# Forget sums and the causal mask of branch B move from TensorE to VectorE; the shift's weights and the key stacks are spread

## The chip, the cores and the metric

One core of one Trainium2 chip runs the whole kernel. The metric is the device time of the execution in microseconds (us); lower is better. The time before is 2265.0 us, the median of three runs.

## The reference

A pool-mixer block is followed by a hybrid layer of three attention branches: A (sliding window, 12 heads), B (forgetting attention, 12 heads) and C (attention over 256 memory tokens, 4 heads). There are 512 tokens, the width is 2048, and everything is fp32. Cut to what matters:

```python
def first_block(x, c, w_mod, b_mod, pool_w_in, pool_w_grp, pool_scale, pool_w_out, ...):
    shift, scale, gate = ada_modulation(c, w_mod[i], b_mod[i])   # silu(c) @ w_mod + b_mod, in three parts
    h = rms_norm(x) * (1.0 + scale) + shift
    y = pool_mixer(h, pool_w_in[j], pool_w_grp[j], pool_scale[j], pool_w_out[j])
    x = x + gate * y
    return rms_norm(x) * final_norm_g
...
def forgetting_attention(q, k, v, f_logit, q_gain, k_gain):       # branch B, 12 heads of 64
    log_f = jax.nn.log_sigmoid(f_logit.astype(jnp.float32))
    c = jnp.cumsum(log_f, axis=1).transpose(0, 2, 1)
...
    def block_fn(args):
        sc = jnp.einsum('bqhd,bshd->bhqs', qb, k) * scale + cqb[..., None] - c[:, :, None, :]
        mask = key_pos[None, :] <= qpos[:, None]
        sc = jnp.where(mask[None, None], sc, NEG)
        p = jax.nn.softmax(sc, axis=-1)
        return jnp.einsum('bhqs,bshd->bqhd', p, v)
...
def hybrid_layer(x, mem, ...):
    proj = rms_norm_2(x, norm_gain) @ w_in
    ua = (sliding_window_attention(...) * silu(za)) @ w_branch_a
    ub = (forgetting_attention(...) * silu(zb)) @ w_branch_b
    uc = (memory_attention(...) * silu(zc)) @ w_branch_c
    g = sigmoid(gate_logits)
    return x + (g0 * ua + g1 * ub + g2 * uc) @ w_out
```

For B the score of a query and a key is their product, plus the query's running sum of log forget values, minus the key's, with all later keys masked out. The query's sum is the same for all keys of one softmax row.

## The kernel before

Every fp32 product is made of three matmuls on split numbers: a weight piece of 128 x 512 comes from memory as `raw`, ScalarE casts it to `whi` (line 91), VectorE subtracts to get `wlo` (line 92), and TensorE multiplies high by high, high by low and low by high (`mm3`, all through line 257). All weights go through one stream (`Stream`): a list of entries (`plan`), loaded in order by SyncE into 3 `raw` buffers of 512 KB. Half an entry is one piece. Four `whi`/`wlo` pairs exist, two more are lent in the first third of the program, and `take` keeps two pieces ready ahead of the one being used (four while the pairs are lent). Entries with a key are not split: VectorE multiplies them by `csil` and adds them up (`gemv`, `shift_part`, `gate_part`).

The order of all engines is the program order, written out by hand. The main loop (`tile_steps`) calls `step()` after every three matmuls of a piece (about 0.7 us); a projection of 8 tiles has 64 such steps. `step` adds a rate to a credit, and each whole credit runs a side generator on to its next `yield` (an advance). `drain()` runs what is left of it at once. So attention is a generator beside the projections of the next heads: `attend` for C, for A (two units of 6 heads) and for B (three units of 4 heads), each beside two projections (for the last B unit beside the first two gate tiles) at a rate of 0.4 (0.34 for C).

A B unit runs in this order. `silu_z`; `head_norm` (9 advances, with a Sqrt on ScalarE); four stacks (`transp_stack`, lines 879 to 894), two of queries and two of keys, each an advance: four transposes into a PSUM bank, then ScalarE and VectorE write high and low halves from the same bank. The bank alternates (`S4[2 + nside % 2]`); before the first B unit 18 stacks and splits have gone by, so a B unit's four stacks take banks s2, s3, s2, s3. Then come 12 items, three to a head, with 128 + 256, 384 and 512 key columns. Item `e` has `s0(e)` in one advance (scores in bank s0 or s1: two matmuls for the products, one with `cs` and `mov` for both forget sums, one with `idr` and `dmr` for the mask; VectorE takes the row maximum, line 1078; ScalarE does the Exp straight from PSUM, line 1083) and `s2(e)` three advances later (transposes of `pt` into bank s2; ScalarE writes `pth`, VectorE `ptl`, lines 1130 and 1132). After a head's last item `s4` multiplies by the values into bank s3, `release` (lines 1023, 1024) reads that bank one advance later at the start of the next loop pass, ahead of `s0`, `finish` scales, and `flush` transposes the finished pair of heads into the score bank that the next item uses.

Ahead of attention: the modulation. `mod` loads the scale part of `w_mod`, VectorE adds it up (line 441), and the first `w_pin` tiles wait for it. The 32 entries of the shift part (`plan_shift`, 512 KB each, line 653) stand in the plan behind those tiles: 2, and then 2 behind every `w_pin` tile of groups 2 and 3. `begin_shift` needs the last of them in the last tile of group 3. At lines 812 to 828 the pool `a3` opens, and its small constants are loaded and copied.

## Time and profile before

| | us |
|---|---|
| three runs | 2263.77, 2265.0, 2267.54 |
| median | 2265.0 |
| profiled execution, its time | 2263.53 |
| its span in the trace | 2261.7 |
| TensorE busy | 2211.3 |
| VectorE busy | 1146.0 |
| ScalarE busy | 873.4 |
| mean granted TensorE clock | 0.993 |

The span is the time from the first to the last instruction of the profiled execution; 1.8 us of its time lie outside of it. Matmuls overlap in the records, so a busy TensorE may still run late: the start of one matmul to the start of the next is the better measure, and 178 or 179 matmuls of 512 columns in 40 us is what it does undisturbed.

### The profile page before, as it was taken

To read this page: it belongs to the slowest core of one execution; us is meant where nothing else is said; L and a number is where in the kernel's file an instruction comes from. 1 tells how busy PE (TensorE), PEld (TensorE's weight loads), DVE (VectorE), ACT (ScalarE), POOL (GpSimd) and SP (SyncE) were. 2 spreads that over 40 slices of the span, in tenths; PEclk is the share of its full clock that TensorE was granted. 3 is DMA by queue.
4 is the path that set the end of the run, shared out by engine and by line. 5 is a ranking of instruction groups with operands and counts; after the bars stand their busy time and mean duration, and the time that the engine had idled before them with its cause. 6 is when DMAs were issued, how large, how long until landed. Compare 5 with 4: busy or idle time off the path is not lost.

```text
span 2261.7 us, 26823 instructions
## 1 busy us (share of the span) xinstructions
PE 2211.3 (98%) x10199; PEld 1820.7 (80%) x10199; DVE 1146.0 (51%) x1996; ACT 873.4 (39%) x1707; POOL 0.2 (0%) x4
## 2 busy tenths in 40 slices
PE   7999999999999999999999999999999999999999
PEld 4678788888888988888878787788888888888887
DVE  3655675436665354657564645554334235326332
ACT  4432263333334353545454546442232222224221
POOL 0000000000000000000000000000000000000000
PEclk9999999999999999999999999999999999999999
DMA  9836743336764332222222222233333333333443
GB/s 328 279 102 199 239 122 111 94 121 225 226 220 126 101 91 75 75 75 75 75 75 75 75 75 75 66 96 100 93 93 102 96 101 93 102 95 98 154 131 112
DMA packets 164665, 275.12 MB, mean 122 GB/s; under 512 B 11074, under 2 KB 62776, under 8 KB 164280
## 3 DMA queue, kind: packets, MB, share of 16 engines
q1 hardware_dynamic: 164536, 273.41, 39.6%
q8 instruction: 80, 1.31, 0.2%
q14 instruction: 49, 0.40, 0.1%
HBM read 264.98 MB, written 8.39 MB: 121 GB/s over the span
## 4 chain that ended last, share of the span: by engine, by line
PE 82%; DVE 7%; DMA 6%; ACT 4%; issue 2%; SPq 0%; ACTq 0%; DVEq 0%
PE m L257 54%; PE s L257 25%; DMA raw<-w_pin 2%; DVE wlo L92 1%; DVE qk L893 1%; DMA raw<-w_kv 1%; ACT whi L91 1%; PE s L1105 1%; DMA raw<-w_pout 1%; ACT pt L1083 1%; ACT qk L889 1%; DMA raw<-w_mod 1%; DVE acc L441 1%; DVE nm L1076 1%; DVE pt L1074 0%
## 5 line engine op out<-in xcount | busy, mean ns | idle before, releaser
L92 DVE TENSOR_TENSOR wlo<-raw,whi 128x512 fp32r<-128x512 f32 (+2 forms) x740 | 493.2, 675 | 770.9 <-ACT whi L91 761.2
L91 ACT CAST whi<-raw 128x512 fp32r<-128x512 f32 (+2 forms) x740 | 441.0, 608 | 878.5 <-PE m L257 385.4
L257 PE MATMUL m<-whi,h_h 128*128 128x512 f32 (+2 forms) x960 | 372.8, 388 | 4.4 <-ACT whi L91 2.9
L257 PE MATMUL m<-wlo,h_h 128*128 128x512 f32 (+2 forms) x960 | 362.2, 377 | 2.1 <-DVE wlo L92 2.0
L257 PE MATMUL m<-whi,h_l 128*128 128x512 f32 (+2 forms) x960 | 362.6, 378 | 0.0
L257 PE MATMUL m<-h_h,whi 128*128 128x512 f32 x768 | 305.8, 398 | 4.9 <-ACT up L549 3.4
L257 PE MATMUL m<-h_h,wlo 128*128 128x512 f32 x768 | 302.6, 394 | 2.2 <-DVE wlo L92 2.2
L257 PE MATMUL m<-h_l,whi 128*128 128x512 f32 x768 | 302.2, 393 | 0.0
L257 PEld LDWEIGHTS m<-whi,h_h 128*128 128x128 f32 x960 | 180.9, 188 | 31.9 <-ACT whi L91 3.4
L257 PEld LDWEIGHTS m<-whi,h_l 128*128 128x128 f32 x960 | 180.6, 188 | 31.6
L257 PEld LDWEIGHTS m<-wlo,h_h 128*128 128x128 f32 x960 | 181.1, 189 | 28.6 <-DVE wlo L92 2.9
L257 PE MATMUL s<-h_h,wlo 128*128 128x512 f32 x512 | 200.1, 391 | 0.0
L257 PE MATMUL s<-h_h,whi 128*128 128x512 f32 x512 | 200.0, 391 | 0.0
L257 PE MATMUL s<-h_l,whi 128*128 128x512 f32 x512 | 200.0, 391 | 0.0
L257 PEld LDWEIGHTS m<-h_h,whi 128*128 128x128 f32 x768 | 146.2, 190 | 35.5 <-ACT up L549 3.8
L257 PEld LDWEIGHTS m<-h_h,wlo 128*128 128x128 f32 x768 | 146.1, 190 | 34.4 <-DVE wlo L92 3.0
L257 PEld LDWEIGHTS m<-h_l,whi 128*128 128x128 f32 x768 | 146.4, 191 | 29.8
L257 PEld LDWEIGHTS s<-h_h,whi 128*128 128x128 f32 x512 | 96.7, 189 | 20.1
L257 PEld LDWEIGHTS s<-h_l,whi 128*128 128x128 f32 x512 | 96.5, 189 | 20.1
L257 PEld LDWEIGHTS s<-h_h,wlo 128*128 128x128 f32 x512 | 96.5, 189 | 20.1
L257 PE MATMUL m<-whi,y_h 128*128 128x512 f32 x256 | 102.6, 401 | 1.7 <-DVE t L777 1.7
L257 PE MATMUL m<-whi,y_l 128*128 128x512 f32 x256 | 99.9, 390 | 0.0
(237 smaller groups left out, 2731.2 us busy)
## 6 DMA issues: line engine op xcount, KB each, us to landing
raw<-w_mod SPq DMA_DIRECT2D x96, 512.0 KB, 4.6
raw<-w_in SPq DMA_DIRECT2D x96, 512.0 KB, 3.8
raw<-w_pin SPq DMA_DIRECT2D x58, 512.0 KB, 3.7
raw<-w_in SPq DMA_DIRECT2D x96, 256.0 KB, 3.1
raw<-w_pout SPq DMA_DIRECT2D x32, 512.0 KB, 4.4
raw<-w_out SPq DMA_DIRECT2D x32, 512.0 KB, 3.7
raw<-w_in SPq DMA_DIRECT2D x32, 384.0 KB, 3.4
raw<-w_kv SPq DMA_DIRECT2D x16, 512.0 KB, 6.9
```

Of the source, the lines that this page charges most:

```text
L91: self.nc.scalar.copy(h3, v)
L92: self.nc.vector.tensor_tensor(out=l3, in0=v, in1=h3.bitcast(F32), op=ALU.subtract)
L257: PE.matmul(ps, lhsT=lhsT, rhs=rhs, start=start, stop=stop)
L441: V.scalar_tensor_tensor(out=acc, in0=v[:, e, :], scalar=w, in1=acc, op0=mult, op1=add)
L889: S.activation(hi[r, :], b[r, :], AF.Copy, scale=gain[r, :])
L893: V.scalar_tensor_tensor(out=outs[e][1][w, :], in0=b[r, :], scalar=gain[r, :], in1=r32(hi[r, :]), op0=mult, op1=sub)
L1076: V.tensor_reduce(out=s["nm"][:, qt : qt + m], in_=w, axis=AX.X, op=vmax)
L1083: S.activation(pt[:, c0 : c0 + n], (pt if kind == "A" else b)[:, c0 : c0 + n], AF.Exp, bias=s["nm"][:, qt : qt + 1], accum_out=s["den"][:, ...
L1105: PE.transpose(b[:, x * P : (x + 1) * P], pt[:, c : c + P], idf)
```

## The change

- B's two score matmuls for the sums and the mask are gone. VectorE adds the key's sums (`sums`) to the scores as it takes them out of PSUM, and the mask (`dmf`) to the last 128 columns; maximum and Exp then read `pt` in SBUF. The query's sum is left out, since it cancels in the softmax.
- The key's sums come once per head from one 128 x 512 matmul (`key_sums`, bank s3) with a column selector (`pick`), copied to SBUF by ScalarE. `key_sums(0)` has an advance of its own behind the stacks; `key_sums(h + 1)` is issued in `s0` of a head's last item. The copies to `idr`, `dmr` and the scaled `cs` (line 967) are gone, and `ct2` with them.
- A key stack takes two advances in place of one. `flush` moves from the second to the first advance of a loop pass, ahead of `finish`, and one advance earlier. The rate is 0.41 in place of 0.4 for A and B.
- `silu_z` ends with an Exp on one column.
- The shift's 32 entries are spread: 10 behind the first `w_pin` tiles, 2 behind the strided entries, 10 in group 2, 10 in group 3. The accumulators move to a pool that lives longer, and `xr` takes their place later.

```diff
@@ -145,9 +145,6 @@
     for kp in range(8):
         for c in range(2):
             ent(w_kv, kp, [(512 * c, 512, 0)])
-    for kp in range(8):
-        ent(w_pin, kp, [(0, 512, 0)])
-        ent(w_pin, kp, [(512, 384, 0)], n=384)
 
     shifts = [(k, c) for k in range(NK) for c in range(2)]
 
@@ -156,24 +153,28 @@
             ent(w_mod, 0, [(1024 * c, 1024, 0)], n=1024, kc=1, row0=k * P, key=("s", c, k))
         del shifts[:n]
 
+    for kp in range(8):
+        ent(w_pin, kp, [(0, 512, 0)])
+        ent(w_pin, kp, [(512, 384, 0)], n=384)
+        plan_shift((0, 0, 1, 1, 2, 2, 2, 2)[kp])
     for r in range(2):
         ent(w_pin, 0, [(896, 128, 0)], n=128, kc=8, row0=1024 * r)
-    plan_shift(2)
+        plan_shift(1)
 
 
     GRP = {2: {2: (0, 0), 5: (0, 1)}, 3: {2: (1, 0), 5: (1, 1)}, 4: {3: (2, 0), 6: (2, 1)}, 5: {3: (3, 0), 6: (3, 1)}}
 
-    def plan_group(w, segs, n=512, grp={}, gate=None, shift=0):
+    def plan_group(w, segs, n=512, grp={}, gate=None, shift=None):
         for kp in range(8):
             if gate is not None:
                 ent(w_mod, kp, [(4096 + 512 * gate, 512, 0)], key=("g", gate, kp))
             ent(w, kp, segs, n=n)
-            plan_shift(shift)
+            plan_shift(shift[kp] if shift else 0)
             if kp in grp:
                 ent(w_grp, 0, [(0, 512, 0)], row0=512 * grp[kp][0] + 256 * grp[kp][1])
 
     for g in range(2, 8):
-        plan_group(w_pin, [(512 * g, 512, 0)], grp=GRP.get(g, {}), shift=2)
+        plan_group(w_pin, [(512 * g, 512, 0)], grp=GRP.get(g, {}), shift={2: (2, 1, 1, 1, 2, 1, 1, 1), 3: (2, 1, 2, 1, 2, 1, 1, 0)}.get(g))
     for cg in range(4):
         plan_group(w_pout, [(512 * cg, 512, 0)], gate=cg)
     CG = [(5120, 346), (5466, 346), (5812, 344)]
@@ -329,6 +330,16 @@
     xnT = [xq[k // 4][:, k % 4, :] for k in range(NK)]
     st.lend(yhs.enter_context(tc.tile_pool(name="hlx", bufs=2)))
 
+    sacc = [yhp.tile([P, 1024], F32, tag=f"sacc{c}", name=f"sacc{c}") for c in range(2)]
+
+    def shift_part(c, k, v):
+        w, v = csil[:, k : k + 1], v[:, 0, :]
+        if k == 0:
+            V.tensor_scalar(out=sacc[c], in0=v, scalar1=w, scalar2=None, op0=mult)
+        else:
+            V.scalar_tensor_tensor(out=sacc[c], in0=v, scalar=w, in1=sacc[c], op0=mult, op1=add)
+
+
     p0 = ExitStack()
     a0 = p0.enter_context(tc.tile_pool(name="a0", bufs=1))
     mod = Stream(nc, mod_plan, p0.enter_context(tc.tile_pool(name="gp", bufs=9)), None, 9, 0)
...
@@ -643,16 +654,6 @@
                     pool[0] = new_pool(i + cp, 1 - cp)
 
 
-    sacc = [a1.tile([P, 1024], F32, tag=f"sacc{c}", name=f"sacc{c}") for c in range(2)]
-
-    def shift_part(c, k, v):
-        w, v = csil[:, k : k + 1], v[:, 0, :]
-        if k == 0:
-            V.tensor_scalar(out=sacc[c], in0=v, scalar1=w, scalar2=None, op0=mult)
-        else:
-            V.scalar_tensor_tensor(out=sacc[c], in0=v, scalar=w, in1=sacc[c], op0=mult, op1=add)
-
-    more["s"] = shift_part
     shf = a1.tile([P, NK], F32, name="shf")
 
     shifted = [0]
@@ -785,7 +786,9 @@
             if kp == 6:
                 drain()
                 for tt in range(NT):
-                    xr = a2.tile([P, 512], F32, tag=f"xr{tt}", name="xr")
+                    if tt % 2 == 0:
+                        two = yhp.tile([P, 2, T], F32, tag=f"sacc{tt // 2}", name="xr")
+                    xr = two[:, tt % 2, :]
                     nc.sync.dma_start(xr, x[tt * P : (tt + 1) * P, cg * 512 : (cg + 1) * 512])
                     xrs.append(xr)
             if kp == 7:
@@ -811,16 +814,12 @@
     ur = [uraw_p.tile([P, T], F32, tag=f"ur{k}", name=f"ur{k}") for k in range(NK)]
     p3 = ExitStack()
     a3 = p3.enter_context(tc.tile_pool(name="a3", bufs=1))
-    idr = a3.tile([P, P], F32R, name="idr")
-    S.copy(idr, idf)
     dmf = a3.tile([P, P], F32, name="dmf")
     nc.sync.dma_start(dmf, dmask)
-    dmr = a3.tile([P, P], F32R, name="dmr")
-    S.copy(dmr, dmf)
     rels = a3.tile([P, 256], F32, name="rels")
     nc.sync.dma_start(rels, rel)
-    csl = a3.tile([P, 12], F32, name="csl")
-    nc.sync.dma_start(csl, csel)
+    ckl = a3.tile([P, 12], F32, name="ckl")
+    nc.sync.dma_start(ckl, csel)
     snk = a3.tile([P, 12], F32, name="snk")
     nc.sync.dma_start(snk, sinks.partition_broadcast(P))
     bfg = a3.tile([P, 12], F32, name="bfg")
@@ -891,14 +890,14 @@
                 S.activation(hi[o, :], b[r, :], AF.Copy, scale=gain[r, :])
             for w in ((r, o) if keys else (o,)):
                 V.scalar_tensor_tensor(out=outs[e][1][w, :], in0=b[r, :], scalar=gain[r, :], in1=r32(hi[r, :]), op0=mult, op1=sub)
-        yield
+            if e or keys:
+                yield
 
     qk12 = a3.tile([P, 12, T], F32R, name="qk12")
     qkh, qkl = qk12[:, 0:6, :], qk12[:, 6:12, :]
     vhl = a3.tile([P, 2048], F32R, name="vhl")
 
     mov = a3.tile([P, T], F32R, name="mov")
-    ct2 = a3.tile([P, T], F32R, name="ct2")
 
     def forget(qk):
         lf = a3.tile([P, 512], F32, tag="pt", name="lf", bufs=2).rearrange("p (t h) -> p t h", t=NT)
...
@@ -930,12 +929,9 @@
         for tt in range(NT):
             mm(b[:, tt * P :], lf[:, tt, :], trs[:, : T - tt * P], start=tt == 0, stop=tt == NT - 1)
         yield
-        V.memset(r32(mov), 1.0)
-        V.memset(r32(ct2), 1.0)
+        V.memset(r32(mov), 0.0)
         S.copy(mov[0:64, :], b[0:64, :])
         V.tensor_tensor(out=mov[32:64, :], in0=b[32:64, :], in1=r32(mov[32:64, :]), op=sub)
-        S.copy(ct2[64:128, :], b[64:128, :])
-        V.tensor_tensor(out=ct2[96:128, :], in0=b[96:128, :], in1=r32(ct2[96:128, :]), op=sub)
         yield
 
     def split_v(srcs, dst, d):
@@ -954,6 +950,8 @@
         def silu_z():
             z = vz[:, :, zoff : zoff + nh * d]
             S.activation(z, z, AF.Silu)
+            t = a3.tile([P, 1], F32, tag="tab", name="tab", bufs=2)
+            S.activation(t, ones[:, 0:1], AF.Exp)
 
         hs = {}
 
@@ -962,13 +960,27 @@
                 s = {}
                 s["nm"] = a3.tile([P, NT], F32, tag="nm", name="nm", bufs=3)
                 s["den"] = a3.tile([P, NT], F32, tag="den", name="den", bufs=3)
-                if kind == "B" and "cs" not in s:
-                    s["cs"] = a3.tile([P, T], F32R, tag="cst", name="cst", bufs=2)
-                    S.activation(s["cs"], r32(ct2), AF.Copy, scale=csl[:, h0 + h : h0 + h + 1])
                 hs[h] = s
             return hs[h]
 
+        sel, sums = {}, {}
+
+        def pick(h):
+
+            sel[h] = a3.tile([P, P], F32R, tag="sel", name="sel", bufs=2)
+            S.activation(sel[h], ones, AF.Copy, scale=ckl[:, h0 + h : h0 + h + 1])
+
+        def key_sums(h):
+
+
+            b = bank("s3")
+            mm(b, sel.pop(h), mov, start=True, stop=True)
+            sums[h] = a3.tile([P, T], F32, tag="cst", name="cst", bufs=2)
+            S.copy(sums[h], b)
+
         head_state(0)
+        if kind == "B":
+            pick(0)
 
         if kind == "C":
             vv = vhl.rearrange("p (m h e) -> p m h e", m=2, h=4)
@@ -1056,12 +1068,13 @@
                     mm3(bb, qkh[:, h, qs], qkl[:, h, qs], kch[:, h, ks], kcl[:, h, ks], True, True)
                 else:
                     mm(bb, qk12[:, h, qs], kh[:, ks], start=True)
-                    mm(bb, qk12[:, h, qs], kl[:, ks], stop=kind != "B")
-                if kind == "B":
-                    mm(bb, s["cs"][:, qs], mov[:, :n])
-                    mm(b[:, c0 + n - P : c0 + n], idr, dmr, stop=True)
+                    mm(bb, qk12[:, h, qs], kl[:, ks], stop=True)
             if segs[0][0] == 0 and h + 1 < nh:
                 head_state(h + 1)
+                if kind == "B":
+                    pick(h + 1)
+            if kind == "B" and segs[-1][0] == NT - 1 and h + 1 < nh:
+                key_sums(h + 1)
             pt = a3.tile([P, 512], F32, tag="pt", name="pt", bufs=2)
             its[e] = pt
             q0, nq = segs[0][0], len(segs)
@@ -1074,13 +1087,19 @@
                     V.scalar_tensor_tensor(out=w, in0=rels[:, 256 - n :].unsqueeze(1).to_broadcast([P, m, n]), scalar=SLOPES[h0 + h],
                                            in1=v, op0=mult, op1=add)
                     V.tensor_reduce(out=s["nm"][:, qt : qt + m], in_=w, axis=AX.X, op=vmax)
+                elif kind == "B":
+                    w = pt[:, c0 : c0 + m * n]
+                    V.tensor_tensor(out=w, in0=b[:, c0 : c0 + m * n], in1=sums[h][:, :n], op=add)
+                    dg = pt[:, c0 + n - P : c0 + n]
+                    V.tensor_tensor(out=dg, in0=dg, in1=dmf, op=add)
+                    V.tensor_reduce(out=s["nm"][:, qt : qt + m], in_=w, axis=AX.X, op=vmax, negate=True)
                 else:
                     V.tensor_reduce(out=s["nm"][:, qt : qt + m], in_=v, axis=AX.X, op=vmax, negate=True)
             if kind == "A":
                 nm = s["nm"][:, q0 : q0 + nq]
                 V.tensor_scalar(out=nm, in0=nm, scalar1=snk[:, h0 + h : h0 + h + 1], scalar2=-1.0, op0=vmax, op1=mult)
             for qt, c0, n in segs:
-                S.activation(pt[:, c0 : c0 + n], (pt if kind == "A" else b)[:, c0 : c0 + n], AF.Exp, bias=s["nm"][:, qt : qt + 1],
+                S.activation(pt[:, c0 : c0 + n], (b if kind == "C" else pt)[:, c0 : c0 + n], AF.Exp, bias=s["nm"][:, qt : qt + 1],
                              accum_out=s["den"][:, qt : qt + 1])
 
 
@@ -1159,25 +1178,28 @@
 
             for q in pend:
                 q[2] += 1
-            if pend and (force or pend[0][2] > 1):
+            if pend and (force or pend[0][2] > 0):
                 un, chunk, _, os = pend.pop(0)
                 b = bank(S4[(e + 1) % 2])
                 for tt in range(NT):
                     PE.transpose(b[:, tt * P : (tt + 1) * P], un[:, tt, :], idf)
                 V.tensor_tensor(out=ur[chunk], in0=b, in1=os, op=mult)
 
+        if kind == "B":
+            key_sums(0)
+            yield
         ne = len(items)
         for e in range(ne + 2):
             for h in later:
                 release(h)
             if e < ne:
                 s0(e)
+            flush(e)
             while later:
                 finish(later.pop(0))
             yield
             if e >= 2:
                 s4(e - 2)
-            flush(e)
             if 1 <= e <= ne:
                 s2(e - 1)
             yield
@@ -1254,7 +1276,7 @@
         proj(qk2, False)
         vz2 = new_vz()
         proj(vz2, True)
-        aside(attend(kind, unit, qk2, vz2), 0.4)
+        aside(attend(kind, unit, qk2, vz2), 0.41)
 
 
     p4 = ExitStack()
...
```

## Rows read from the trace of the kernel before

**Rows 1.** The page's list of engines: busy us (share of the span) x instructions.
```profile
PE 2211.3 (98%) x10199; PEld 1820.7 (80%) x10199; DVE 1146.0 (51%) x1996; ACT 873.4 (39%) x1707; POOL 0.2 (0%) x4
```

**Rows 2.** The view by windows, three stretches of 40 us: group 2 to group 3 of the pool block, the start of the last B unit, and the gate tiles. Columns: stretch, length, busy us (x instructions) of each engine, granted clock, DMA share, GB/s.
```profile
240.00:280.00 40.00, 36.59 (x154) 29.72 (x153) 26.51 (x29) 12.06 (x21) 0.00 (x0) 0.96 0.72 232
...
1360.00:1400.00 40.00, 36.77 (x164) 29.29 (x163) 26.13 (x49) 23.69 (x46) 0.00 (x0) 0.91 0.28 78
1520.00:1560.00 40.00, 40.00 (x179) 33.10 (x178) 21.13 (x32) 9.12 (x15) 0.00 (x0) 1.00 0.36 104
```

**Rows 3.** The view of waits, TensorE, whole span: who waited for whom, us in total, times, longest.
```profile
PE colb L257 <- DVE acc L441: 7.3, 6, 2.7
...
PE s L257 <- DVE ur L1167: 3.3, 2, 1.6
```

**Rows 4.** The timeline of TensorE in the second B unit: start us, us, instruction, count. Scores of a head's first item (128 and 256 columns), of its last item (512 columns), and of the next head's last item.
```profile
1265.80 0.28 PE L257 MATMUL s<-mov,cst 128*128 128x128 f32 x1
...
1266.02 0.46 PE L257 MATMUL s<-qk 128*128 128x256 f32 x2
1266.31 0.28 PE L257 MATMUL s<-mov,cst 128*128 128x256 f32 x1
...
1266.49 0.45 PE L257 MATMUL m<-whi,h_h 128*128 128x512 f32 x1
...
1280.35 0.39 PE L257 MATMUL s<-mov,cst 128*128 128x512 f32 x1
...
1280.64 0.45 PE L257 MATMUL m<-whi,h_h 128*128 128x512 f32 x1
...
1295.39 0.39 PE L257 MATMUL s<-mov,cst 128*128 128x512 f32 x1
```

**Rows 5.** The timeline around the end of group 2, TensorE and ScalarE, and the group of the shift's sums on VectorE in the view by lines from 178 to 306 us (busy us, mean ns, idle before).
```profile
247.87 0.39 PE L257 MATMUL m<-h_h,wlo 128*128 128x512 f32 x1
251.67 0.50 PE L257 MATMUL m<-h_h,whi 128*128 128x512 f32 x1 [3.41 <-ACT up L549]
...
249.99 1.14 ACT L91 CAST whi<-raw 128x512 fp32r<-128x512 f32 x2 [3.53 <-DMA raw<-w_pin]
...
L653 DVE SCALAR_TENSOR_TENSOR sacc<-raw,csil,sacc 128x1024 f32<-128x1024 f32 x30 | 37.8, 1281 | 8.4 <-DMA raw<-w_mod 8.4
```

**Rows 6.** The timeline where the pool `a3` opens: ScalarE's copy of the mask, and TensorE's next matmul behind it.
```profile
726.18 0.30 ACT L819 CAST dmr<-dmf 128x128 fp32r<-128x128 f32 x1 [2.57 <-DMA dmf<-dmask]
...
726.91 0.43 PE L257 MATMUL m<-whi,h_h 128*128 128x346 f32 x1 [1.41 <-ACT whi L91]
```

**Rows 7.** The view by lines, ScalarE's table loads ahead of a Sqrt (L310) and of the first Exp of an attention unit (L1083): count, busy us, mean ns, idle before.
```profile
L310 ACT ACT_TABLE_LOAD x8 | 10.3, 1283 | 0.1
L1083 ACT ACT_TABLE_LOAD x8 | 10.3, 1283 | 5.8 <-DVE nm L1078 5.8
```

**Rows 8.** The view of waits, TensorE, 1127 to 1470 us (the three B units).
```profile
PE s L1105 <- ACT pt L1083: 5.4, 3, 3.5
PE m L257 <- ACT whi L91: 2.9, 2, 1.5
PE m L257 <- DVE wlo L92: 2.1, 2, 1.2
```

**Rows 9.** The timeline at the start of the second B unit: transposes of its last key stack, the first scores, the last piece of that stack on ScalarE and VectorE, and TensorE's transposes of the first `pt`.
```profile
1263.53 0.60 PE L885 MATMUL s<-idf,qk 128*128 128x128 f32 x4
...
1265.36 0.60 PE L257 MATMUL s<-qk 128*128 128x128 f32 x2
...
1270.85 0.68 ACT L889 ACTIVATE qk<-s,cols 64x512 fp32r<-64x512 f32 x1 [1.81 <-DVE qk L893]
...
1272.26 1.53 DVE L893 SCALAR_TENSOR_TENSOR qk<-s,cols,qk 64x512 fp32r<-64x512 f32 x2 [1.45 <-ACT qk L891]
...
1276.31 1.15 PE L1105 MATMUL s<-idf,pt 128*128 128x128 f32 x3 [3.49 <-ACT pt L1083]
```

**Rows 10.** The items of the second B unit, 1280 to 1340 us (four heads): the stretch in the view by windows (columns as in group 2), then groups of the view by lines for VectorE and ScalarE; the last two groups are branch A's scores plus bias, taken from PSUM, in 1015 to 1127 us.
```profile
1280.00:1340.00 60.00, 60.00 (x313) 50.97 (x312) 34.00 (x78) 29.96 (x82) 0.00 (x0) 1.00 0.26 76
...
L92 DVE TENSOR_TENSOR wlo<-raw,whi 128x512 fp32r<-128x512 f32 x18 | 12.3, 691 | 10.5 <-ACT whi L91 10.2
L1132 DVE TENSOR_TENSOR ptl<-s,pth 128x128 fp32r<-128x128 f32 x24 | 7.0, 290 | 8.3 <-ACT pth L1130 8.3
...
L1130 ACT CAST pth<-s 128x128 fp32r<-128x128 f32 x24 | 6.4, 265 | 10.2 <-DVE ptl L1132 8.3 <-PE s L1105 2.0
...
L1130 ACT CAST pth<-s 128x256 fp32r<-128x256 f32 x7 | 2.6, 372 | 4.5 <-PE s L1105 3.1 <-DVE ptl L1132 1.4
...
L1023 ACT COPY os<-s 64x512 f32<-64x512 f32 x4 | 2.3, 580 | 2.1 <-PE s L257 2.0
...
L1074 DVE SCALAR_TENSOR_TENSOR pt<-rels,s 128x512 f32<-128x512 f32 x6 | 4.1, 677 | 0.0
...
L1074 DVE SCALAR_TENSOR_TENSOR pt<-rels,s 128x128 f32<-128x128 f32 x6 | 1.7, 280 | 0.1
```

**Rows 11.** The timeline of the first B unit where a head's output bank is read: TensorE in the second head's last scores, VectorE's `release` of the first head.
```profile
1180.15 0.40 PE L257 MATMUL s<-mov,cst 128*128 128x512 f32 x1
...
1181.21 0.68 DVE L1024 TENSOR_TENSOR os<-s,os 64x512 f32<-64x512 f32 x1 [0.55 <-ACT os L1023]
```

More of the change, by code (lines that the diff above doesn't have):

```diff
@@ L425, in _build @@
     accs = {}
-    more = {}
+    more = {"s": shift_part}
     def gemv(key, v):
@@ L606, in ev @@
             if b % 2 == 0:
-                two = a1.tile([P, 2, T], F32, tag=f"sacc{b // 2}", name="sg")
+                two = yhp.tile([P, 2, T], F32, tag=f"sacc{b // 2}", name="sg")
                 sgs.extend((two[:, 0, :], two[:, 1, :]))
@@ L923, in forget @@
         V.scalar_tensor_tensor(out=lf[:, :, 0:12], in0=xl, scalar=0.0, in1=el, op0=vmin, op1=sub)
-        for q in (32, 64, 96):
+        for q in (32,):
             V.tensor_copy(lf[:, :, q : q + 12], lf[:, :, 0:12])
@@ L1375, in host_arrays @@
         csel[[h, 32 + h], h] = -1.0
-        csel[[64 + h, 96 + h], h] = 1.0
     edge = np.ones((4, 2, 8), np.float32)
```

## Prediction

> **What bounds the kernel now.** I read the page's engine list first [rows 1]: TensorE is busy 2211 of 2262 us, VectorE half of the time, ScalarE 39%. So a change can gain in three ways only: matmuls that go, stops of TensorE, and stretches at its low clock. Next the windows [rows 2]: a stretch of gate tiles does 179 matmuls of 512 columns in 40 us (0.2235 us each, granted clock 1.00). Two others stand below that: 240 to 280 us with 154 matmuls at 0.96, and 1360 to 1400 with shorter matmuls at 0.91; behind a stop the clock runs at 1.2 GHz for a few us before it is back at 2.4. Then the waits of TensorE for what the change could touch: 7.3 us in the modulation and 3.3 us for `ur`, the flush [rows 3]; 5.4 + 2.9 + 2.1 = 10.4 us in the three B units [rows 8]. Last the timelines around each edit. The kernel is TensorE's except where a chain of VectorE and ScalarE briefly falls behind it, and the question of the change is whether it makes those chains longer than it makes TensorE's work shorter.
>
> **TensorE's work in B.** [rows 4] give it by spacing of starts. At 128 columns the `mov,cst` matmul starts at 1265.80 and the next product at 1266.02: 0.22 for sums and mask. At 256: 1266.31 to 1266.49, 0.18. At 512: 1280.35 to 1280.64, 0.29. For 384 I take 0.24, between its neighbours. Together 0.93 a head, 12 heads: 11.2 us go. `key_sums` adds one matmul of 512 columns a head, 0.23 (undisturbed rate, [rows 2]): 2.8. **Net -8.4 us**, if TensorE sets the pace.
>
> **The chain of the items.** Does it? One head took 1295.39 - 1280.35 = 15.0 us [rows 4]; less 8.4/12 = 0.7, TensorE wants 14.3. In 1280 to 1340 us VectorE is busy 34.0 of 60 us [rows 10], which looks like room. But its idle time is ended by ScalarE: 10.5 us before `wlo` and 8.3 before `ptl`, and ScalarE's in turn by VectorE, 8.3 before `pth`. The two engines wait in turn for each other, in program order, and what counts is the chain they form. What it has in hand is the time that ScalarE waits for TensorE: 2.0 + 3.1 (`pth`) + 2.0 (`os`) = 7.1 us for four heads, 1.8 a head. So the chain needs 15.0 - 1.8 = 13.2 a head now. The change puts the adds into it: `tensor_tensor` from PSUM to SBUF has its nearest row in branch A's score plus bias, 0.28 for 128 columns and 0.677 for 512 [rows 10]; between these 0.41 for 256 and 0.55 for 384: 0.28 + 0.41 + 0.55 + 0.68 = 1.92 a head. The mask adds are 128 columns each, 4 x 0.28 = 1.12. For ScalarE I take 0.15: the copy of `sums` (0.58 for 512 columns, as the `os` copy, [rows 10]) and `pick` come, the scaled `cs` goes. Sum 3.2, so 16.4 a head, where before it was 15.0: **+1.4 a head**. I count this for 9 heads, +12.6, since the last head of a unit has the time up to the next projection to catch up; the other 3 give 0.7 each, -2.1. **Net +10.5 us** with TensorE's saving in it. Bounds: all adds hidden, -8.4; all 12 heads, +16.8. I choose nearer to the upper end because the adds stand between the scores and the Exp, ahead of all that the next steps wait for, and VectorE's `wlo` for the main matmuls queues behind them. A part of this is `key_sums(h + 1)`, which takes bank s3 while `release` still reads it: in [rows 11] VectorE's `release` ended at 1181.21 + 0.68 = 1181.89, while TensorE did the scores of that item at 1180.15, so this matmul waits about 1.7 us, with main matmuls queued behind it on TensorE.
>
> **The start of a B unit.** Now the last key stack's transposes start at 1263.53 and the first scores follow at 1265.36, but the stack's last VectorE piece ends at 1272.26 + 1.53 = 1273.8; ScalarE and VectorE take the one bank in turn (1.81 and 1.45 us of waiting) [rows 9]. TensorE pays for it later, in the 3.49 wait for `pt`. In pieces, `key_sums(0)` comes two advances of about 1.7 us (4 tiles' matmuls of three at the rate 0.4: 0.68 / 0.4) behind 1265.36, at 1268.8. It needs bank s3, which the unit's fourth stack still holds: 1273.8 - 1268.8, 5.0 less some 0.3 for the smoother pieces: 4.7 us, three units, +14. The 10.4 us of old waits [rows 8] go, since what came late was late by that same 5 us. **Net +3.6**; bounds -10.4 (the pieces bring VectorE up to TensorE) and +15 (full wait, and a part of the old waits stays).
>
> **The shift.** TensorE stops from 247.87 to 251.67, 3.41 us of it waiting, behind ScalarE that waited 3.53 us for a `w_pin` piece [rows 5]: the 512 KB entries of the shift come two behind every tile there and fill the 3 `raw` buffers. Behind the stop the low clock costs about 1.7 us more (0.96 for 40 us, [rows 2]). With 22 entries over 16 steps in place of 32 and ten earlier, both go, as nothing else is shown late there: -5.1 to -5.4, **-5.4**; 0 if the stop only moves. The sums are 1.28 us of VectorE each [rows 5]; two or more of them now run beside the modulation, where VectorE's column sums hold TensorE for 7.3 us [rows 3]: two in front of the last column sum cost 2.6, a half of it hidden, **+1.2** (0 to 4).
>
> **Smaller edits.** Without the copies `idr` and `dmr` ScalarE no longer waits 2.57 us for the mask's DMA ahead of `whi`; TensorE waited 1.41 there [rows 6]: **-1.5** (0 to -1.5). VectorE now reads `dmf` much later. `flush` one advance earlier frees the 3.3 us [rows 3], but its transposes then follow the scaled pair `un` more closely, and `ur` runs ahead of `finish`: **-1.7** (-3.3 to +1). The rate 0.41 shortens an advance by 2.4%: 0.04 us, nothing beside the waits, and it moves no step past a tile.
>
> **The Exp on one column** (`silu_z`). It loads the table early so that the items' first Exp needs no load. The rows: ScalarE loads a table ahead of a Sqrt 8 times (L310) and ahead of a first Exp 8 times (L1083), 1283 ns each [rows 7], and in a unit the order is Silu, Sqrt (`head_norm`), Exp. An Exp between Silu and Sqrt cannot keep its table past the Sqrt, so each unit of A and B, and C, six in all, gets one load more on ScalarE, in front of the main `whi`: 1.28, of which I take 0.8 as not hidden: **+5** (0 to 9).
> The Trainium skill (ScalarE: Activation LUTs, section "Table sets: the hidden batching unit") says that Exp and Sqrt lie in different sets and that going from one to the other and back takes two loads; the trace's 8 and 8 agree. The same page, section "What ACT_TABLE_LOAD costs", gives 2.66 us a switch with its drain, where the rows show 1.28; by it the six would be 16 us of ScalarE, an estimate, and the sum some 8 us higher.
>
> **The sum.** 10.5 + 3.6 - 5.4 + 1.2 - 1.5 - 1.7 + 5 = +11.7 us. On the profiled execution, 2263.5: 2275.2. The median of the runs is 1.5 above that execution: **2277 us**, 0.5% slower.
>
> **Rivals.** (a) **VectorE has room.** It is busy 57% in the items [rows 10]; with 3.0 us more a head it stands at 11.5 of 14.3, and if ScalarE and VectorE drift apart so that neither waits in turn, the chain hides. It decides when the chain takes less than TensorE's 14.3 us a head. Then -8.4 - 10.4 + 3 (key sums at the starts, 1 us each) - 5.4 - 1.5 - 3.3 = -26: 2239 us. For it: the share of VectorE; against it: nearly all idle of VectorE ends with ScalarE.
> (b) **The pieces free the start.** The main `whi` and `wlo` now come between the halves of a stack, TensorE's waits go and `key_sums(0)` finds its bank free: -10.4 in place of +3.6, the rest as above, -2.3: 2262.7 us, no change. Against it: VectorE was 8.4 us late and pieces give it two advances, 3.4.
> Section "Optimizing Scalar/DVE Operations" of Perfetto Trace Analysis in the Trainium skill speaks for (b): "If Scalar/Vector aren't saturated, but are causing bubbles on other engines, breaking up instructions may allow work to be completed sooner." Here instructions aren't broken up, only parted by others; no run so far shows it.
> (c) **The spread doesn't do what it says.** The ten early entries and denser groups move the stop to where the other weights need the buffers: +5.4 on my sum, 2282 us.
>
> **Chances.** My forecast 0.51, (c) 0.12, (b) 0.14, (a) 0.23. This kernel's runs can tell about 0.2%, 4.5 us. So slower 0.63, same 0.14, faster 0.23. The likeliest case's own range is 2268 to 2290, by the bounds of the items and the table loads; to hold 8 in 10 the range must take in (b) and some of (a): 2248 to 2290.
>
> **What would show it.** Right: waits of TensorE at the `mov,sel` matmul, for VectorE's `qk` (5 us at each unit's start) and `os`; head spacing of 16 us; six more table loads; no stop near 248. Wrong: head spacing of 14.3 us and TensorE's waits in B under 5 us (then the chain hid), or table loads unchanged in count, or a new stop of 3 us before 240.

## The result, and the profile after

The changed kernel takes 2293.6 us (median of 4 runs, 2290.59 to 2295.82) against 2265.8 of the one before in all its runs with it: ratio 1.0125 [1.0113, 1.0138], some 28 us slower. Forecast were 2277 us and a range up to 2290: the sign was right, the loss is more than twice the 11.7 us of the sum, and it lies 3.6 us above the range. The profiled execution took 2290.59 us, its span is 2288.8.

The list of engines after (busy us, share of the span, instructions) answers to [rows 1]:

```profile
PE 2209.7 (97%) x10115; PEld 1815.6 (79%) x10115; DVE 1181.5 (52%) x2088; ACT 886.8 (39%) x1728; POOL 0.2 (0%) x4
```

VectorE has 35.5 us more. The adds themselves took 37.1 us, 3.09 a head, where the prediction had 3.04; the mask's are this line of the view by lines after:

```profile
L1094 DVE TENSOR_TENSOR pt<-pt,dmf 128x128 f32<-128x128 f32 x48 | 14.0, 292 | 1.6
```

TensorE is busy for nearly as long as before, in a span that is 27 us longer: it waits.

The view of waits after, TensorE, 880 to 1520 us (branches A and B: who waited for whom, us in total, times, longest), answers to [rows 3, 8]:

```profile
PE s L258 <- DVE os L1036: 18.7, 6, 6.7
PE s L258 <- DVE qk L892: 16.0, 3, 5.4
PE s L1185 <- DVE un L1049: 6.5, 4, 2.1
PE s L1124 <- DVE ptl L1151: 3.0, 3, 1.0
PE s L258 <- DVE ptl L1151: 2.6, 4, 0.8
PE s L884 <- DVE qk L858: 2.3, 2, 1.1
PE s L873 <- DVE qk L892: 1.6, 3, 0.9
PE s L258 <- ACT pth L1149: 1.2, 1, 1.2
PE m L258 <- DVE wlo L92: 0.3, 2, 0.2
```

These are 52.2 us; in the kernel before the same stretch has 18.0. The two long rows are the waits that the prediction looked for: the key's sums wait for `release` (`os`, six times) and for the last key stack (`qk`, three times). The old waits for `pt` and `whi` [rows 8] are gone.

The first B unit after, in the timeline (start us, us, instruction, idle before): the last key stack's transposes, VectorE's last pieces of that stack, and the first sums, which answer to [rows 9]; then the 512-column scores of four heads and two of the sums' waits, which answer to [rows 4, 11]:

```profile
1149.21 0.60 PE L884 MATMUL s<-idf,qk 128*128 128x128 f32 x4
...
1156.89 1.53 DVE L892 SCALAR_TENSOR_TENSOR qk<-s,cols,qk 64x512 fp32r<-64x512 f32 x2 [0.72 <-ACT qk L890]
...
1158.57 0.77 PE L258 MATMUL s<-mov,sel 128*128 128x512 f32 x1 [5.31 <-DVE qk L892]
...
1170.11 0.63 PE L258 MATMUL s<-qk 128*128 128x512 f32 x2
...
1185.85 0.63 PE L258 MATMUL s<-qk 128*128 128x512 f32 x2
...
1188.59 0.68 DVE L1036 TENSOR_TENSOR os<-s,os 64x512 f32<-64x512 f32 x1
...
1189.41 0.47 PE L258 MATMUL s<-mov,sel 128*128 128x512 f32 x1 [2.93 <-DVE os L1036]
...
1204.83 0.63 PE L258 MATMUL s<-qk 128*128 128x512 f32 x2
...
1207.53 0.47 PE L258 MATMUL s<-mov,sel 128*128 128x512 f32 x1 [2.07 <-DVE os L1036]
...
1221.13 0.62 PE L258 MATMUL s<-qk 128*128 128x512 f32 x2
```

Read the third row first: 5.31 us for the stack that VectorE ends at 1156.89 + 1.53 = 1158.4, the term that the prediction had at 4.7. Then the spacing of heads: 51.0 us from 1170.11 to 1221.13, 17.0 a head, where [rows 4] have 15.0 for one head and the forecast was 16.4.

The clock, in the view by windows after (stretch, length, busy us (x instructions) of each engine, granted clock, DMA share, GB/s), answers to [rows 2]:

```profile
240.00:280.00 40.00, 40.00 (x178) 33.06 (x177) 28.49 (x35) 13.38 (x22) 0.00 (x0) 1.00 0.67 210
1120.00:1160.00 40.00, 34.53 (x156) 27.75 (x155) 24.56 (x43) 24.88 (x41) 0.00 (x0) 0.95 0.27 79
1160.00:1200.00 40.00, 36.52 (x163) 29.30 (x162) 24.00 (x58) 19.64 (x53) 0.00 (x0) 0.93 0.18 53
1280.00:1320.00 40.00, 34.07 (x148) 27.29 (x149) 23.68 (x57) 19.11 (x49) 0.00 (x0) 0.91 0.22 66
1400.00:1440.00 40.00, 28.76 (x122) 22.44 (x120) 22.15 (x47) 22.25 (x47) 0.00 (x0) 0.90 0.19 53
1440.00:1480.00 40.00, 35.83 (x172) 29.75 (x172) 26.83 (x64) 19.70 (x52) 0.00 (x0) 0.93 0.18 53
```

240 to 280 us is whole again: 178 matmuls, no stop. In B the five stretches shown stand below full clock. 0.95 over 40 us is 0.05 x 40 = 2.0 us of full speed that was not granted; the five make (0.05 + 0.07 + 0.09 + 0.10 + 0.07) x 40 = 15.2 us. A part of that lies in the stops themselves. The granted clock in finer slices shows six stretches of 1.2 GHz with TensorE at work, 3.9, 3.4, 2.9, 3.3, 5.9 and 3.7 us long; half of their 23.0 us is lost, 11.5. In B before there are two, 3.3 and 6.0 us: 4.6. How one begins can be seen behind the second unit's first sums:

```profile
1282.45 0.76 PE L258 MATMUL s<-mov,sel 128*128 128x512 f32 x1 [5.28 <-DVE qk L892]
1283.01 0.63 PE L258 MATMUL m<-whi,h_h 128*128 128x512 f32 x1
1283.44 0.63 PE L258 MATMUL m<-wlo,h_h 128*128 128x512 f32 x1
...
1285.48 0.40 PE L258 MATMUL m<-whi,h_h 128*128 128x512 f32 x1
1285.71 0.40 PE L258 MATMUL m<-wlo,h_h 128*128 128x512 f32 x1
```

After 5.28 us of standing the matmuls come every 0.43 us (1.2 GHz) for some 3 us, then every 0.23 (2.4 GHz).

Where the 27 us came from, by the start of the n-th `whi` cast on ScalarE (740 in both traces, in the same order, counted from 0):

| cast | before | after | difference | what lies up to it |
|---|---|---|---|---|
| 90th | 338.2 | 332.6 | -5.5 | modulation, shift |
| 240th | 752.4 | 744.3 | -8.1 | rest of the pool block, opening of `a3` |
| 290th | 889.1 | 881.0 | -8.1 | branch C |
| 360th | 1133.2 | 1133.3 | +0.1 | branch A |
| 460th | 1487.9 | 1514.9 | +27.1 | branch B |
| end | 2261.7 | 2288.8 | +27.1 | gates and output |

From the 290th to the 460th cast 35.2 us are lost. Waits make 52.2 - 18.0 = 34.2, the clock 11.5 - 4.6 = 6.9, the saved matmuls -8.4 (the prediction's estimate): together 32.7.

### The profile page after: what moved, and what is told of

Read it like the earlier page. It is cut to its first block, busy times and chain, and to the rows that moved or that the text cites. A ratio compares the mean times of both kernels' runs of the same rounds, so it can differ in the third digit from the quotient of the medians.

```text
span 2288.8 us, 26744 instructions
## 1 busy us (share of the span) xinstructions
PE 2209.7 (97%) x10115; PEld 1815.6 (79%) x10115; DVE 1181.5 (52%) x2088; ACT 886.8 (39%) x1728; POOL 0.2 (0%) x4
## 4 chain that ended last, share of the span: by engine, by line
PE 76%; DVE 11%; ACT 7%; DMA 3%; issue 2%; SPq 0%; ACTq 0%; DVEq 0%
PE m L258 50%; PE s L258 25%; DVE wlo L92 3%; ACT whi L91 1%; ACT pt L1102 1%; DVE ptl L1151 1%; DVE qk L892 1%; DMA raw<-w_kv 1%; DVE nm L1095 1%; ACT pth L1149 1%; DMA raw<-w_pout 1%; DVE pt L1092 1%; ACT qk L888 1%; DVE nm L1089 1%; DVE pt L1094 1%
```

## The experiments

**Two theories** on branch B came first. Theory 1, the bank: the long waits are there because `key_sums` takes bank s3 while a stack or `release` still reads it; the sums elsewhere in the order, and they are gone. Theory 2, the lag: VectorE and ScalarE are that late in any case, and TensorE would meet the lag at its next use of their work. Each result is given with its ratio to the kernel before on the same chip; differences between kernels that ran on different chips are taken from these ratios, times 2265.8.

**The shift alone** (the first seven pieces of the diff, on the kernel before).

> The kernel before with the shift's entries spread and its accumulators moved, nothing else. Both theories on branch B say the same of it: up to the 80th weight piece the changed kernel was 5.5 us ahead of the one before (by the starts of ScalarE's casts), so 2260 against 2265.8, with no stop of TensorE near 248 us. If the gain is given back behind the pool block, it shows no difference.

Measured 2260.5 us, 0.9976 [0.9966, 0.9985]: 5.4 us gained, and kept to the end. The spread does what it says.

**The sums taken early.**

```diff
                 if kind == "B":
-                    pick(h + 1)
-            if kind == "B" and segs[-1][0] == NT - 1 and h + 1 < nh:
-                key_sums(h + 1)
+                    key_sums(h + 1)
+                    if h + 2 < nh:
+                        pick(h + 2)
...
-        if kind == "B":
-            key_sums(0)
-            yield
         ne = len(items)
```

with `key_sums(0)` and its `yield` ahead of the first stack, and `pick(1)` beside `pick(0)`.

> The changed kernel with the key's sums taken at other points of the order: the unit's first ahead of the four stacks, the next head's in a head's first item in place of its last one (and the selector a head earlier). Work and banks are the same. Theory 1 (the bank): TensorE's waits at the sums' matmul, 18.7 us for os and 16.0 for qk, come from bank s3 alone; they go with the low clock behind them, and the time falls by 25 to 40 us, to 2254 to 2268. Theory 2 (the lag): VectorE and ScalarE are that late in any case because of the adds; TensorE waits for pt, ptl and pth instead, and the time falls by 10 us at most.

Measured 2287.4 us, 1.0098 [1.0083, 1.0113]: only 6.1 us less. TensorE's waits in 880 to 1520 us:

```profile
PE s L258 <- DVE qk L892: 13.1, 3, 4.4
PE s L1128 <- DVE ptl L1155: 12.3, 7, 2.6
PE s L1189 <- DVE un L1053: 7.9, 6, 2.2
PE s L258 <- DVE ur L1190: 3.6, 3, 1.4
```

The 18.7 us for `os` are gone, and 12.3 for `ptl`, with more for `ur` and `un`, stand in their place: the lag. But the second head's sums still met the fourth stack in s3 (13.1), so the start was not tested yet.

**The first two sums ahead of the stacks** (in the loop over the stacks: `if h < 2: key_sums(h)`, and an advance behind the first; later heads as in the run above).

> The changed kernel with the sums of a unit's first two heads ahead of its stacks, and the others in the first item of the head before. In the run with the sums taken early (2287), the next head's sums were still asked for while bank s3 held the fourth stack, and TensorE waited 13.1 us for qk there. Now no sums meet a bank in use. Theory 1 (the bank): those 13.1 us and their low clock go, 2265 to 2274. Theory 2 (the lag): TensorE waits for pt and ptl at the start of the items in their place, as the kernel before did for 10.4 us: 2280 to 2288.

Measured 2289.7 us, 1.0115 [1.0100, 1.0129]: no gain on the run above, 2.3 us less than the changed kernel, and just above what theory 2 expected. Now no long wait at a sums' matmul is left, and the longest waits are

```profile
PE s L1131 <- DVE ptl L1158: 15.3, 10, 2.6
PE s L1192 <- DVE un L1056: 8.3, 7, 2.2
PE s L884 <- ACT cst L979: 5.0, 3, 1.9
PE s L1131 <- ACT pt L1109: 4.4, 6, 0.9
```

A new one, 5.0 us for the copy of the sums, stands at the stacks (this order has its own price). Theory 1 has fallen: the two orders gained 6.1 and 2.3 us, not 25 to 40. TensorE also worked less at 1.2 GHz here, 13.6 us in 880 to 1520 us where the changed kernel has 23.0, and that hardly shows in the time either.

**The same without the mask's adds** (the line `V.tensor_tensor(out=dg, in0=dg, in1=dmf, op=add)` left out; later keys are not masked).

> As the run with the first two sums ahead of the stacks, and without VectorE's adds of the causal mask: 4 of 0.28 us a head, 13.4 us of VectorE in all, left out (later keys count). Theory 2 (the lag: what VectorE does between scores and Exp is on the path): 10 to 20 us below that run, with the waits for ptl. Theory 1: within 4 us of it.

Measured 2271.8 us, 1.0032 [1.0019, 1.0046]: 17.9 us below the run above, on the same chip, for 14.0 us of VectorE (48 adds of 0.292). These adds, between scores and Exp, are on the path at their full length, and some low clock with them: TensorE's work at 1.2 GHz in 880 to 1520 us fell from 13.6 to 6.8 us, half of which is 3.4. Theory 2 stands.

**Flush back, and no Exp on one column**, each alone on the changed kernel.

> The changed kernel with flush back in the second advance of the pass and one pass later. If flush's new place costs what TensorE's waits for un show (6.5 us in 4) and with it branch A's loss of about 8 us between the 290th and 370th piece, the time falls by 4 to 8 us, to 2286 to 2290; the old waits for ur (3.3 us) come back. If the table loads are what costs in A, it stays within 2 us.

> The changed kernel without the Exp on one column. Six table loads of 1.28 us go from ScalarE. My forecast counted 0.8 us for each: 5 us less, 2288.6. If they are hidden, no difference.

Flush back: 2296.1 us, 1.0134 [1.0119, 1.0149], no faster (2 us slower, within the intervals): where 6.5 us of waits for `un` went, 3.8 for `ur` and longer ones for `ptl` came. No Exp: 2289.4 us, 1.0104 [1.0089, 1.0118], 4.7 us less, though the intervals just touch. ScalarE's loads in the changed kernel's view by lines (count, busy us, mean ns, idle before):

```profile
L311 ACT ACT_TABLE_LOAD x8 | 10.3, 1283 | 0.1
L1102 ACT ACT_TABLE_LOAD x8 | 10.3, 1283 | 0.9 <-DVE nm L1095 0.8
...
L954 ACT ACT_TABLE_LOAD x6 | 7.7, 1283 | 0.0
```

Six new ones at L954, the 8 and 8 of [rows 7] unchanged: none was saved. (Left out between them: the loads of L952, Silu, six as before.)

**What the other edits are worth on their own**, built up on the kernel before with the spread: first the mask's copy moved from the opening of `a3` to `forget`, then each key stack in two advances.

> The kernel before with the shift spread, and ScalarE's copy of the mask moved from the opening of the pool to forget, long behind its DMA; B's scores stay on TensorE. The changed kernel gained 2.1 us at that place. Expected 2.1 less than with the spread alone: 2258.4.

> As the run with the mask's copy later, and each key stack in two advances. If the pieces let the main pieces' whi and wlo in between (my rival b), TensorE's 10.4 us of waits at the starts of the B units go, 5 to 10 us below that run, 2249 to 2254. If VectorE is as late as before, no difference.

```diff
             for w in ((r, o) if keys else (o,)):
                 V.scalar_tensor_tensor(out=outs[e][1][w, :], in0=b[r, :], ...)
-        yield
+            if e or keys:
+                yield
```

Copy later: 2256.5 us, 0.9968 [0.9955, 0.9980], 1.8 us below the spread alone, though the intervals overlap. Pieces: 2245.1 us, 0.9916 [0.9902, 0.9930], 11.4 us below that on the same chip, more than was expected. In 880 to 1520 us TensorE's longest waits are now

```profile
PE s L258 <- DVE ur L1171: 3.3, 2, 1.6
PE s L1109 <- DVE ptl L1136: 2.0, 1, 2.0
PE s L1109 <- ACT pt L1087: 1.5, 2, 0.7
```

The first is branch A's, as before; of the 10.4 us in [rows 8] only the 1.5 for `pt` and 0.2 for `wlo` are left, with 2.0 for `ptl` beside them. All of TensorE's waits in 880 to 1520 us fell from 17.0 to 9.6 us, and its work at 1.2 GHz there from three stretches, 15.2 us, to one of 3.4: 7.4 us of waits and 5.9 of clock, 13.3 of the 13.5 us by which the two traces differ between their 290th and 460th casts. By this count nearly half of the gain is the low clock.

**Rate and flush on that version.**

> As the run with the key pieces (2245), with the rate 0.41 in place of 0.4 for A and B. In the changed kernel branch A lost some 8 us against the one before, in units where only the rate, flush and the table load differ; without the table load it lost 4.4. If the rest is the rate's, 3 to 6 us slower, 2248 to 2251; my prediction put the rate at nothing.

> As the run with the key pieces, with flush in the changed kernel's place and an advance earlier. My prediction: 1.7 us less (3.3 less to 1 more). If TensorE's waits for un are what A pays, 3 to 6 us more, 2248 to 2251.

Rate 0.41: 2251.6 us, 0.9935 [0.9923, 0.9948], 4.3 us slower by the ratios (their intervals overlap a little), 6.5 by the medians; TensorE's waits in 880 to 1520 us went from 9.6 to 16.6 us. Flush early: 2243.1 us, 0.9901 [0.9887, 0.9914], 2 us less by the medians and 3.4 by the ratios, which the intervals don't part from none. It has 5.6 us of waits for `un`, and those for `ur` are gone.

**The move alone**: the changed kernel with the first two sums ahead of the stacks (without the extra advance), without the Exp on one column, and with rate and flush of before; only sums and mask set it apart from the run with the pieces. And the same with the mask on TensorE.

> The changed kernel with the first two sums ahead of the stacks, without the table load, with flush and the rate of before: against the run with the key pieces (2245), only the sums and the mask on VectorE differ. Theory 2 (the lag): the adds, 3.04 us of VectorE a head, 36.5 in all, cost 20 to 35 us net of TensorE's saving: 2265 to 2280. If the other edits (rate, flush, table) were the larger part of the loss, 2245 to 2255.

> As the run with the move alone, with the mask back on TensorE (idr and dmr, 4 matmuls of 128 columns a head) and VectorE adding the sums only; nothing is left out. The run without mask adds gained 17.9 us. Theory 2: 13 to 18 us below the run with the move alone, after 1 to 3 us for the matmuls. If the two engines' hops and not VectorE's time are what counts, within 5 us of it.

```diff
-                    mm(bb, qk12[:, h, qs], kl[:, ks], stop=True)
+                    mm(bb, qk12[:, h, qs], kl[:, ks], stop=kind != "B")
+                if kind == "B":
+                    mm(b[:, c0 + n - P : c0 + n], idr, dmr, stop=True)
...
-                    V.tensor_tensor(out=dg, in0=dg, in1=dmf, op=add)
```

The move alone: 2270.7 us, 1.0025 [1.0016, 1.0034], 24.7 us above the run with the pieces by the ratios. With the mask on TensorE (and the copies `idr` and `dmr` back) 2256.6 us, 0.9957 [0.9944, 0.9969], 14.1 below the move alone, though TensorE has 48 matmuls more. The waits for `ptl` in 880 to 1520 us are, in the one and in the other,

```profile
PE s L1127 <- DVE ptl L1154: 19.8, 18, 3.2
```
```profile
PE s L1131 <- DVE ptl L1158: 8.9, 12, 2.8
```

The first and the fourth head's 512-column scores of the first B unit, in the run with the pieces, with the mask on TensorE, and in the move alone:

```profile
1157.54 0.62 PE L258 MATMUL s<-qk 128*128 128x512 f32 x2
...
1203.25 0.63 PE L258 MATMUL s<-qk 128*128 128x512 f32 x2
```
```profile
1157.51 0.63 PE L258 MATMUL s<-qk 128*128 128x512 f32 x2
...
1205.41 0.62 PE L258 MATMUL s<-qk 128*128 128x512 f32 x2
```
```profile
1159.48 0.62 PE L258 MATMUL s<-qk 128*128 128x512 f32 x2
...
1211.19 0.62 PE L258 MATMUL s<-qk 128*128 128x512 f32 x2
```

That is 45.7, 47.9 and 51.7 us: 15.2, 16.0 and 17.2 a head. The low clock has no part in it, as the view by windows shows (columns as above) for the run with the pieces, the move alone and the changed kernel:

```profile
1130.00:1510.00 380.00, 375.86 (x1824) 312.80 (x1823) 211.82 (x416) 201.20 (x433) 0.00 (x0) 1.00 0.27 80
```
```profile
1130.00:1510.00 380.00, 348.89 (x1620) 278.23 (x1619) 239.34 (x499) 197.67 (x430) 0.00 (x0) 1.00 0.25 73
```
```profile
1130.00:1510.00 380.00, 339.51 (x1562) 274.92 (x1561) 233.55 (x493) 198.34 (x432) 0.00 (x0) 0.96 0.23 67
```

The first two have one stretch at 1.2 GHz each, 3.4 us long. The sum of waits, clock and saved matmuls that came out for the changed kernel doesn't do so here: 36.4 - 9.6 = 26.8 us of waits, no clock and -8.4 make 18.4, and the traces differ by 27.1 between the 290th and the 460th cast. So that sum is no proof of its terms.

**What was left open by then**: the parts didn't add up to the changed kernel's loss, by 7 us or more. Two more runs tried the rate.

> The changed kernel with the rate back at 0.4 and nothing else. With the kernel's scores on TensorE the rate 0.41 cost 6.5 us. If the rate's cost is the advances' pace against a chain that can't follow, it costs as much or more here: 6 to 14 us less, 2280 to 2287. If TensorE waits for the chain anyway, whatever the pace, the rate changes nothing here and some 10 us of the loss stay unexplained.

> The kernel before with the spread shift, the later mask copy, the key pieces and flush early (2243), at the rate 0.39. If slower advances give VectorE and ScalarE time, the waits for un and ptl (8.6 us) shrink and it gains 2 to 5 us; if what is left over at the last tile of the projections is then run at once, with nothing between, it loses 5 us or more.

The changed kernel at 0.4: 2285.0 us, 1.0081 [1.0066, 1.0096], 10 us less by the ratios, 8.6 by the medians. The fastest version at 0.39: 2245.6 us, 0.9904 [0.9888, 0.9921], no different from 0.4, which neither case of the expectation had. So 2.5% faster advances cost 4 to 10 us, and slower ones bring nothing where the scores are on TensorE. The changed kernel was not run below 0.4, though its heads take 17 us in place of 15: what its move costs at a pace that this longer chain can follow is not known.

The fastest of all was the kernel before with the spread, the later copy, the pieces and flush early, at 2243 us: 1.0% below the one before, 2.2% below the changed one.

## Why the prediction went wrong, point by point

**The bound, and the sign: right.** The items are set by the chain through VectorE and ScalarE, not by TensorE, and busy shares hid it: with VectorE 57% busy its adds were nearly all on the path. Rival (a) fell with the mask's adds (17.9 us for 14.0 of VectorE).

**The rate: the step that failed most clearly.** "0.04 us, nothing beside the waits, and it moves no step past a tile" was wrong: 8.6 to 10 us in the changed kernel, and 4.3 with the scores on TensorE, where the intervals overlap a little. It explains half of branch A's loss of 8.2 us, where the forecast had about nothing: from the 290th to the 360th cast the changed kernel takes 252.3 us at 0.41 and 248.5 at 0.4, the version with the pieces 248.6 and 244.5. The other half is the Exp on one column: the changed kernel without it takes 248.8, the kernel before 244.1. Each advance was priced by its length. That a chain with no slack can't follow a faster pace is the likely reason; how the advances fall between the pieces' steps may matter too, and no run parts the two. Why 0.39 gives nothing back is open with it.

**The clock in B: a term that was missing.** The low clock behind a stop was counted for the stop near 248 us that goes, and at nothing for the stops that come. Six stretches at 1.2 GHz in B, where two were before, are 6.9 us of TensorE's work. Whether they cost the kernel as much is not shown: the pieces gained nearly as much from the clock (5.9 us) as from the waits (7.4), but the move alone costs its 24.7 us with no more low clock than the run that it is compared with.

**The items: right mechanism, too small.** +1.4 a head was forecast; the changed kernel has 17.0 where the unit before took 15.3 (1164.41 to 1210.31 us, three heads): +1.7. Two terms were off. ScalarE's part came to 0.4 a head, not 0.15: `pick` and the copy of the sums (0.40 and 0.59) come for the scaled `cs` (0.725), and the Exp takes longer since it reads `pt` in SBUF, 0.15 for the four of a head, as the 512-column rows of the view by lines show, before and after:

```profile
L1083 ACT ACTIVATE pt<-s,nm 128x512 f32<-128x512 f32 x12 | 8.3, 688 | 15.7 <-DVE nm L1078 15.7
```
```profile
L1102 ACT ACTIVATE pt<-pt,nm 128x512 f32<-128x512 f32 x12 | 8.7, 723 | 13.7 <-DVE nm L1095 13.5
```

And the slack of 1.8 a head, read from ScalarE's waits for TensorE [rows 10], was somewhat too large: 3.5 us in the chain raised the head by 2.0 in the move alone, so 1.5 could be used. The six waits for `os` came to 18.7 us, not 6 x 1.7: [rows 11] showed `release` in a kernel without the adds. One of the six took 6.7 us, in the last B unit; what made it so long is open.

**The start: right in its waits** (16.0 us for 14, the old 10.4 gone); the low clock behind them, 6.3 us, was not in the +3.6, but the old starts had 4.6 of it themselves. The runs add that the bank is only where the lag shows: with the sums elsewhere TensorE waited for `ptl` and the copies.

**Rival (b), the pieces: half right**, and the largest gain of the diff: 11.4 us alone. That this is near the 10.4 of [rows 8] is luck, since by the count above the waits gave 7.4 and the clock, which (b) left out, 5.9; and `key_sums(0)` did not find its bank free (16.0 us). The sum held the gain too, but under the new waits, so the two couldn't be seen apart. The sentence of Perfetto Trace Analysis in the Trainium skill (section "Optimizing Scalar/DVE Operations") speaks of instructions broken up; here an advance was broken up and the instructions stayed whole, and work was done sooner all the same, as the 11.4 us show. **Rival (c) fell**: the spread gained 5.4 us. The forecast for it was -5.4 + 1.2 = -4.2, and the working in the text gives 3.41 + 1.7 = 5.1 for the first term.

**Small terms: right**, as far as the intervals tell. Mask copy -1.8 (forecast -1.5), flush -2 to -3.4 (forecast -1.7), table loads +4.7 (forecast +5, 0.8 of each 1.28 not hidden). By the 2.66 us a switch of ScalarE: Activation LUTs (the Trainium skill, section "What ACT_TABLE_LOAD costs") it would have been 16 us of ScalarE, an estimate; the rows show 1.28 each, and the time fell by 4.7 without them. The same page of the Trainium skill (section "Table sets: the hidden batching unit") has Exp and Sqrt in different sets, and the trace agrees: six loads came and none went.

**What stays open.** The parts, each from its own pair of runs, are spread, mask copy, pieces, move, flush, rate, table loads, and the order of the sums against that with the first two ahead, which the move alone has: -5.4 - 1.8 - 11.4 + 24.7 - 2 + 10 + 4.7 + 2.3 = +21.1 of 28.3. The other 7 us are not explained. Each pair is known to some 2 to 5 us, so the noise of eight pairs could hold them; terms that aren't independent could too. Items and start together (+14.1 in the sum) came near what pieces, move and order give (-11.4 + 24.7 + 2.3 = +15.6), in part by luck: the sum lacked the clock that the pieces gained and had the chain's growth too small. So the rate, put at nothing, is the largest single miss that the runs show.

## What to carry to other kernels

Ask of an engine that is not the bound whether its idle time ends with another engine that it takes turns with; if so, its busy share is no room, and work moved onto it lands on the path at nearly its full length. Where TensorE sets the pace, price a stop with the low clock behind it (by the count above 5.9 us of the 13.3 that the pieces gained); where another chain sets it, the clock may cost nothing more. Check a faster pace of side work against the chain that has to follow it. And take a change of several parts apart: here the spread, the later copy, the pieces and the earlier flush won 22 us together, and were buried under the one move that they came with.

## What the runs showed of the hardware

- In B of the changed kernel TensorE stood for 2.9 us twice, and for 5.3, 5.3, 5.4 and 6.7 us, and ran at 1.2 GHz for 2.9 to 5.9 us behind each of these six; behind the stops of 2.1 us at the sums the granted clock stayed at 1.00. The length of the stop alone doesn't tell it: in the run with the pieces 3.4 us at 1.2 GHz came behind a stop of 2.05 us. In the first of the long ones the lower level began within the stop, some 3 us before its end.
- ScalarE's Exp of 128 x 512 took 723 ns from SBUF and 688 from PSUM (12 of each, kernel after and before).
- Six table loads more on ScalarE, 7.7 us of it, cost 4.7 us of the kernel (the intervals just touch), on an engine that is busy 39%.
